# A DiT block with product-key experts on one core: gate steps dealt out one by one, eight one-hot row buffers, and U tiles fed in halves between the W steps

## The chip, the cores and the metric

The kernel runs on one core of a Trainium2 chip. The metric is the device time of one execution in microseconds (us), from the profiler's side of the chip; lower is better. The engines are PE (TensorE, matmul), DVE (VectorE), ACT (ScalarE), POOL (GpSimd) and SP (SyncE, which here only issues loads). Each works off its own queue strictly in order.

## What is computed

A block of a diffusion transformer for 256 tokens of width 2048: adaptive layer norm, a mixer of a gated MLP and a differential attention, and a feed-forward layer of 16384 experts, of which each token takes 16 for each of 8 heads. The change touches only the last. Cut to what matters, the reference is:

```python
def peer_ffn(h, wq, keys, u_tab, v_tab):            # blocks of 128 tokens, 8 heads
    q = (ht @ wq).reshape(128, 8, 2, 128)
    s = einsum('thcd,hcnd->thcn', q, keys)          # scores against 2 x 128 keys a head
    s_a, i_a = top_k(s[:, :, 0], 16); s_b, i_b = top_k(s[:, :, 1], 16)
    top_s, pos = top_k(all 16 x 16 sums of s_a and s_b, 16)
    idx = (i_a * 128 + i_b) at pos                  # expert a * 128 + b
    gate = softmax(top_s)
    act = gelu(einsum('thkd,td->thk', u_tab[idx], ht))
    return einsum('thk,thkd->td', gate * act, v_tab[idx])

x_new = x_new + g2 * peer_ffn(h2, ...)              # g2: sixth part of silu(c) @ w_ada + b_ada
```

## The kernel before

Ahead of the experts the kernel computes adaptive norms, mixer and output projection, some 630 us, which no part of the change touches. Then come three stages.

**Selection** (about 640 to 885 us). The loop over `j` in 0 to 15 makes one half head's query tile an iteration: `q_tile(j)` multiplies two 512 KB halves of `wq[j]` with h2 (48 matmuls, lines 130 to 132, tile z; the first two tiles are made ahead of the loop). `scores` (L812) multiplies the tile of the iteration before with the keys, and `topk` takes its 16 best on DVE (L790 to L798). At every fourth score tile `lookup` turns positions into experts: a chain that goes from DVE to POOL (L866, L870, L879) and back several times, with an exponential on ACT (L846). The iterations in the list `UJ` (0, 2, 4, 5, 7, 8, 9, 11 to 15) also make one U tile, `u_tile`: 128 experts' rows of u_tab times h2 for the first 192 tokens (TD), 16 pairs of matmuls (lines 135 and 136, tiles n and m). So iterations 1, 3, 6 and 10 have none. `xn_rows` writes rows of x back in the first eight iterations (transposes at L713).

In the same loop `adaln_g2` works out the gate vector g2. It has 32 steps of four traced matmuls (L265), one for each half megabyte of w_ada, and a piece is fetched through POOL's queue (L257) into one of two halves of a buffer. The fetch for step n+2 is issued when step n has read its half; a step that is asked for ends by issuing it. From iteration 2 on, two steps are taken in even iterations and three in odd ones, all ahead of `q_tile`.

All weights come through SP's queue into five raw buffers of 512 KB; `split` (L125, L126) makes a high part of each on ACT, a cast, and a low part on DVE, raw minus high. PE needs both. Three buffers of each exist.

**W stage** (about 885 to 1022). For each of the 192 tokens one matmul (L1016) makes a 128 x 128 table of gates, from a one-hot row block `ob` (four tokens at a time, by DVE at L1009 or by ACT at L1006 and L1007) and a one-hot row `pa` times the gate (L1014), which DVE and POOL make in turn. Six `pa` buffers go round. Four tokens fill a bank z, which ACT copies out (L1017); every 16 tokens a megabyte goes to DRAM. Between them U tiles 17 to 31 are made, a whole tile whenever enough tokens have passed, so that both run side by side.

**U and V** (from about 1022). The rest of the U tiles, the product of gates and activations, and the V tiles; the 64 rows of tokens not covered by TD are gathered and worked off on DVE. The output is written at the end.

The order on each engine isn't the order of the code: a list scheduler places instructions by the code's order as priority, by its own estimate of durations, and with splits raised by 400 places (HP). What it made of the code stands below as rows of the order.

Of the kernel before, what the change touches and what calls it, by code (L numbers as in the profile page):

```python
# [10 lines left out]
F32 = mybir.dt.float32  # L11
# [9 lines left out]
P = 128  # L21
# [8 lines left out]
NE = 128  # L30
# [3 lines left out]
LAG = 32  # L34
TB = 16
TD = 192
# [25 lines left out]
WP = 2  # L62
# [6 lines left out]
def dit_block(ctx: ExitStack, tc: tile.TileContext, xT, ctxT, cT, wad1, wada, bada, n1g, n2g,  # L69
# [15 lines left out]
    work = phase.enter_context(tc.tile_pool(name="work_a", bufs=1))  # L85

    def big(shape, dt=F32):
        return bigp.tile(shape, dt, tag="big", name="big")
# [4 lines left out]
    def w1(shape=(P, T), dt=F32):  # L93
        return work.tile(list(shape), dt, tag="w1", name="w1", bufs=4)
# [7 lines left out]
    def z512():  # L102
        return psz.tile([P, 512], F32, tag="z", name="z")
# [16 lines left out]
    def split(src, raw=None):  # L120
        raw = raw or load(src)
        hi = splp.tile([P, 1024], F32R, tag="hi", name="hi")
        lo = splp.tile([P, 1024], F32R, tag="lo", name="lo")
        with tc.high_priority(offset=HP):
            hi_at[0] = S.copy(hi, raw)  # L125
            anchor[0] = V.tensor_sub(lo, raw, hi)  # L126
        return hi, lo

    def mm3(ps, ah, al, bh, bl, first, last):
        mm(ps, ah, bh, start=first, stop=False)  # L130
        mm(ps, ah, bl, start=False, stop=False)  # L131
        mm(ps, al, bh, start=False, stop=last)  # L132

    def mm2(ps, wh, wl, act, first, last, n=T):
        mm(ps[:, :2 * n], wh, act[:, :, :n], start=first, stop=last)  # L135
        mm(ps[:, :n], wl, act[:, 0, :n], start=False, stop=last, skip_group_check=True)  # L136

    def fold(ps, dst, n=T):
        t = w1([P, n])
        S.copy(t, ps[:, n:2 * n])  # L140
        V.tensor_tensor(dst, ps[:, :n], t, op=ALU.add)
# [110 lines left out]
    def adaln_g2(buf):  # L252
        acc = z512()

        def fetch(n):
            if n < 2 * KT:
                G.dma_start(buf[:, n % 2], wada[3, n // 2, n % 2])  # L257

        for n in range(2):
            fetch(n)  # L260
        for n in range(2 * KT):
            k, i = n // 2, n % 2
            for jj in range(2):
                g = 32 * (2 * i + jj)
                mm(acc[g:g + 32, :], cs[:, k, :], buf[:, i, jj * 512:(jj + 1) * 512], start=(k == 0),  # L265
                   stop=(k == KT - 1))
            fetch(n + 2)
            yield
        S.copy(g2s, acc)
# [115 lines left out]
    def tok_chunk(c, tl, nfill):  # L385
        ps = {t: z512() for t in tl}
        for k2 in range(8):
            tok_part(c, k2, tl, ps)
            if k2 % 2:
                fill(3, nfill[k2 // 2])  # L390
        return ps
# [73 lines left out]
    for c in range(2):  # L465
        ps = tok_chunk(2 + c, (0, 1, 2, 3), FV)
# [58 lines left out]
    def feat_half(src, act8, ps, first, last, wide=True, n=T):  # L525
        hi, lo = split(src)
        for kk in range(8):
            wh, wl = hi[:, kk * P:(kk + 1) * P], lo[:, kk * P:(kk + 1) * P]
            f, l = first and kk == 0, last and kk == 7
            if wide:  # L530
                mm2(ps, wh, wl, act8[:, kk], f, l, n)
            else:
                mm3(ps[:, :n], wh, wl, act8[:, kk, 0, :n], act8[:, kk, 1, :n], f, l)

    def feat_chunk(src, act, ps, wide=True, n=T):
        for half in range(2):
            feat_half(src[half], act[half], ps, half == 0, half == 1, wide, n)
# [122 lines left out]
    for g in range(4):  # L660
        ps = {}
        for kh in range(2):
            for jp in (2 * g, 2 * g + 1):
                for i in range(2):
                    j = 2 * jp + i
# [42 lines left out]
    def xn_rows(b):  # L708
        tp = z512()
        for t in range(TT):  # L710
            for i in range(2):
                c = (2 * t + i) * P
                nc.tensor.transpose(tp[:, c:c + P], xn[:, 2 * b + i, t * P:(t + 1) * P], ident)  # L713
        xr = work.tile([P, TT, T], F32, tag="ob", name="xr", bufs=3)
        S.copy(xr, tp.rearrange("p (t d) -> p t d", t=TT))
        nc.scalar.dma_start(xd[:, :, b * T:(b + 1) * T], xr)

    h2 = [big([P, 8, 2, T], F32R) for _ in range(2)]
# [50 lines left out]
    work = phase.enter_context(tc.tile_pool(name="work_b", bufs=1))  # L769
# [30 lines left out]
    def q_tile(j):  # L800
        if j < WP:
            return wqp[j]
        ps = z512()
        feat_chunk(wq[j], h2, ps, False)
        qp = w1()
        S.copy(qp, ps[:, :T])
        return qp
# [77 lines left out]
    def gel_tile(a):  # L885
        if a % NG == 0:
            gel[a // NG] = gep.tile([P, NG, TD], F32, tag="ge", name="ge")
        return gel[a // NG][:, a % NG, :]

    def u_bank(a):  # L890
        return (m512 if a % 2 and a >= len(UJ) else n512)()

    def u_tile(a):
        if a >= NE:
            return
        ps = u_bank(a)
        feat_chunk(ut[a], h2, ps, True, TD)
        fold(ps, gel_tile(a), TD)

    u_next = 0  # L900


# [13 lines left out]
    def topk(j, qp):  # L916
        scores(j, qp)
        if j % 2:
            cands(j // 2)
        if j % 4 == 3:  # L920
            lookup(j // 2 - 1, 2)
            late_rows.append(j // 2 - 1)
        elif j % 4 == 1 and late_rows:
            rows_of(late_rows.pop(0))
# [28 lines left out]
    pend = []  # L953
    g2 = adaln_g2(gb0[:, 1].rearrange("p (i c) -> p i c", i=2))
    for j in range(16):
        if j >= WP:
            for _ in range(2 + j % 2):
                next(g2, None)
        pend.append((j, q_tile(j)))
        if len(pend) > DL:  # L960
            topk(*pend.pop(0))
        if j < 8:
            xn_rows(j)
        if j == 11:
            gb1 = big([P, 2, D])
            gbufs += [gb0[:, 1], gb1[:, 0], gb1[:, 1]]
        if j in UJ:
            u_tile(u_next)
            u_next += 1
# [18 lines left out]
    u_base = u_next  # L988
# [7 lines left out]
    wd = dram.tile([P, TD // TB, NE, TB], F32, tag="wd", name="wd", bufs=1)  # L996
    stg = big([P, 2, NE, TB])
    NTB = TD // TB
    for tb in range(NTB):
        st = stg[:, tb % 2]  # L1000
        for t4 in range(TB // 4):
            t0 = tb * TB + t4 * 4
            ob4 = work.tile([P, 4, P], F32, tag="ob", name="ob", bufs=3)
            if t4 % 2:
                for i in range(4):
                    S.activation(ob4[:, i, :], iota, AF.Abs, scale=-1.0, bias=eT[:, 1, t0 + i:t0 + i + 1])  # L1006
                S.activation(ob4, ob4, AF.Relu, scale=-1.0, bias=1.0)  # L1007
            else:
                V.tensor_tensor(ob4, iota[:, None, :].to_broadcast([P, 4, P]),  # L1009
                                eT[:, 1, t0:t0 + 4, None].to_broadcast([P, 4, P]), op=ALU.is_equal)  # L1010
            ps = z512()
            for i in range(4):
                pa = work.tile([P, P], F32, tag="pa", name="pa", bufs=6)
                (G if i % 2 else V).tensor_scalar(pa, iota, eT[:, 0, t0 + i:t0 + i + 1], eT[:, 2, t0 + i:t0 + i + 1],  # L1014
                                op0=ALU.is_equal, op1=ALU.mult)
                mm(ps[:, i * P:(i + 1) * P], ob4[:, i, :], pa, start=True, stop=True)  # L1016
            S.copy(st[:, :, t4 * 4:t4 * 4 + 4], ps.rearrange("p (t a) -> p a t", t=4))  # L1017
            while u_next < u_base + (t0 + 4) * (LAG - u_base) // TD:
                u_tile(u_next)
                u_next += 1  # L1020
        nc.scalar.dma_start(wd[:, tb], st)

    wts = {}
# [1 line left out]
    def w_load(gr):  # L1025
        if gr >= NE // NG:
            return
        wt = wtp.tile([P, NTB, NG, TB], F32, tag="wt", name="wt")
        nc.scalar.dma_start(wt, wd[:, :, gr * NG:(gr + 1) * NG, :])
        wts[gr] = wt  # L1030
# [27 lines left out]
        with tc.issue_after(hi_at[0].ins):  # L1058
            w_load(gr + 1)

    def u_steps():
        for a in range(u_next, NE):
            ps = u_bank(a)
            for half in range(2):
                feat_half(ut[a][half], h2[half], ps, half == 0, half == 1, True, TD)
                if half:
                    fold(ps, gel_tile(a), TD)
                yield a - 1 + half

    def v_unit(gr, dq, gt, between):  # L1070
        pa, pb = z512(), z512()
        for pr in range(4):
# [9 lines left out]
        return pa, pb  # L1082

    NGR = NE // NG
    w_load(0)
    ws = w_steps(0)
    for i in range(UX):
# [5 lines left out]
            next(ws, None)  # L1093
    phase.close()
    work = phase.enter_context(tc.tile_pool(name="work_c", bufs=1, reuse_waits="tile"))
    us = u_steps()
    done, wst = [0, 0, 0], [None]
    want = [2 * (NE - u_next), 2 * GT - rows_done[0]]

# [19 lines left out]

    for gr in range(NGR):  # L1120
        gt = gts.pop(gr)
        last = gr == NGR - 1
        if last:
# [3 lines left out]
        for dq in range(4):  # L1127
# [3 lines left out]
            ps = v_unit(gr, dq, gt, between)  # L1131
# [109 lines left out]
```

## Time and profile before

| | us |
|---|---|
| median of 3 runs (2083.24 to 2087.3) | 2086.74 |
| the profiled execution's own time | 2087.58 |
| its span, first to last instruction | 2085.7 |
| PE busy in the span | 1974.5 (95%) |
| DVE busy | 1638.9 (79%) |
| ACT busy | 1008.4 (48%) |
| POOL busy | 405.8 (19%) |
| mean granted clock of PE | 0.987 |

In a timeline row stand the start in us, the busy time of the group, the engine, the line, the operation, the tile written and those read, shapes, and the count; a number in square brackets is the time that the engine sat idle ahead of it, and behind the arrow what ended that. PE runs a float32 matmul of this kernel as two records where it isn't in the float32r format (L265, L713, L812, L1016). A granted clock of 1.00 is 2.4 GHz, 0.50 is 1.2 GHz.

### The profile page before, as it was taken

What the parts mean: (1) busy time and instruction counts of PE and PEld (TensorE: products, weight loads), DVE (VectorE), ACT (ScalarE), POOL (GpSimd) and SP (SyncE); (2) the same over time, 40 slices, a digit from 0 to 9 for tenths busy, and PEclk for the clock granted to TensorE, in tenths of its full rate; (3) what the DMA queues carried; (4) which work ended last, traced back from release to release, by engine and by line L of the source; (5) the groups of instructions that cost most, each with busy time, mean ns of one, the idle gap of its engine ahead of it and who ended that gap; (6) DMA issues with size and microseconds to landing.
All of it is one profiled execution on the core that took longest, in us unless ns stands there. A gap on an engine that the chain in (4) does not pass through costs nothing.

```text
span 2085.7 us, 29831 instructions
## 1 busy us (share of the span) xinstructions
PE 1974.5 (95%) x11182; PEld 1638.0 (79%) x11182; DVE 1638.9 (79%) x2344; ACT 1008.4 (48%) x1393; POOL 405.8 (19%) x315
## 2 busy tenths in 40 slices
PE   4999999999998888889999999999999999999998
PEld 1457775566997777888888898989898888888876
DVE  5338657677667677866698999999999899999997
ACT  3224314565556333377655555545554455445543
POOL 0001000000000232177412222222222223232200
PEclk9999999999999999899999999999999999999999
DMA  8787677776566676556799999999999999999984
GB/s 326 268 310 234 203 256 265 235 252 230 195 204 224 225 270 206 171 193 209 240 369 374 375 367 381 383 377 374 374 377 362 368 362 370 388 361 369 399 324 160
DMA packets 173744, 622.03 MB, mean 298 GB/s; under 512 B 17824, under 2 KB 44704, under 8 KB 154528
## 3 DMA queue, kind: packets, MB, share of 16 engines
q1 hardware_dynamic: 119232, 434.16, 58.7%
q0 software_dynamic: 23040, 151.01, 18.6%
q10 hardware_dynamic: 31328, 34.97, 4.9%
q8 instruction: 87, 1.43, 0.3%
q14 instruction: 57, 0.47, 0.1%
HBM read 603.30 MB, written 16.78 MB: 297 GB/s over the span
## 4 chain that ended last, share of the span: by engine, by line
PE 44%; DMA 3%; DVE 3%; issue 1%; ACT 0%; DVEq 0%; ACTq 0%
PE n L135 6%; PE m L135 6%; PE z L131 5%; PE z L130 5%; PE z L132 5%; PE z L1079 5%; PE z L1080 5%; PE n L136 3%; PE m L136 3%; DVE lo L126 2%; DMA raw<-in_vt 2%; DMA raw<-in_ut 1%; ACT hi L125 0%; DVE big L948 0%; DVE big L1155 0%
## 5 line engine op out<-in xcount | busy, mean ns | idle before, releaser
L125 ACT CAST hi<-raw 128x1024 fp32r<-128x1024 f32 x656 | 688.9, 1050 | 886.4 <-PE z L1079 166.1
L126 DVE TENSOR_TENSOR lo<-raw,hi 128x1024 fp32r<-128x1024 f32 x656 | 798.2, 1229 | 273.9 <-ACT hi L125 267.3
L135 PE MATMUL n<-big,hi 128*128 128x384 f32 x1120 | 334.4, 363 | 0.4 <-DVE big L733 0.2
L136 PE MATMUL n<-big,lo 128*128 128x192 f32 x1120 | 285.5, 255 | 6.4 <-DVE lo L126 6.2
L135 PE MATMUL m<-big,hi 128*128 128x384 f32 x928 | 275.5, 361 | 0.0
L130 PE MATMUL z<-hi,big 128*128 128x512 f32 x608 | 248.2, 409 | 4.5 <-DVE vtok L468 3.2
L131 PE MATMUL z<-lo,big 128*128 128x512 f32 x608 | 244.1, 402 | 4.0 <-DVE lo L126 3.8
L132 PE MATMUL z<-hi,big 128*128 128x512 f32 x608 | 240.1, 398 | 0.0
L136 PE MATMUL m<-big,lo 128*128 128x192 f32 x928 | 236.3, 255 | 0.7 <-DVE lo L126 0.7
L136 PEld LDWEIGHTS n<-big,lo 128*128 128x128 f32 x1120 | 216.5, 193 | 12.5 <-DVE lo L126 9.1
L135 PEld LDWEIGHTS n<-big,hi 128*128 128x128 f32 x1120 | 212.7, 190 | 5.4 <-DVE big L733 1.6
L932 POOL DMA_INDIRECT big<-in_vtab,iu x64 | 130.1, 2032 | 364.2 <-DVE big L948 336.7
L136 PEld LDWEIGHTS m<-big,lo 128*128 128x128 f32 x928 | 178.9, 193 | 6.1 <-DVE lo L126 2.9
L932 POOL DMA_INDIRECT big<-in_utab,iu x64 | 108.4, 1694 | 384.3 <-DVE big L940 375.1
L135 PEld LDWEIGHTS m<-big,hi 128*128 128x128 f32 x928 | 175.9, 190 | 3.5
L130 PEld LDWEIGHTS z<-hi,big 128*128 128x128 f32 x608 | 115.4, 190 | 50.8 <-issue 21.7
L130 PE MATMUL z<-big,hi 128*128 128x256 f32 (+1 forms) x512 | 147.9, 290 | 0.0
L948 DVE SCALAR_TENSOR_TENSOR big<-big,gate 128x2048 f32<-128x2048 f32 x63 | 147.7, 2345 | 0.0
L131 PE MATMUL z<-big,hi 128*128 128x256 f32 (+1 forms) x512 | 146.7, 287 | 0.1
L132 PE MATMUL z<-big,lo 128*128 128x256 f32 (+1 forms) x512 | 146.3, 286 | 0.0
L940 DVE SCALAR_TENSOR_TENSOR big<-big 128x2048 f32<-128x2048 f32 x64 | 146.2, 2284 | 0.0
L131 PEld LDWEIGHTS z<-lo,big 128*128 128x128 f32 x608 | 116.0, 191 | 36.3 <-DVE lo L126 9.1
(280 smaller groups left out, 3270.4 us busy)
## 6 DMA issues: line engine op xcount, KB each, us to landing
raw<-in_ut SPq DMA_DIRECT2D x256, 512.0 KB
raw<-in_vt SPq DMA_DIRECT2D x256, 512.0 KB
ra<-in_wada SPq DMA_DIRECT2D x96, 512.0 KB
raw<-in_wkvq SPq DMA_DIRECT2D x64, 512.0 KB
raw<-in_wad SPq DMA_DIRECT2D x42, 512.0 KB
raw<-in_wout SPq DMA_DIRECT2D x32, 512.0 KB
raw<-in_wq SPq DMA_DIRECT2D x32, 512.0 KB
big<-in_wada POOLq DMA_DIRECT2D x32, 512.0 KB, 7.4
```

The lines of the kernel that those rows point to most:

```text
L125: hi_at[0] = S.copy(hi, raw)
L126: anchor[0] = V.tensor_sub(lo, raw, hi)
L130: mm(ps, ah, bh, start=first, stop=False)
L131: mm(ps, ah, bl, start=False, stop=False)
L132: mm(ps, al, bh, start=False, stop=last)
L135: mm(ps[:, :2 * n], wh, act[:, :, :n], start=first, stop=last)
L136: mm(ps[:, :n], wl, act[:, 0, :n], start=False, stop=last, skip_group_check=True)
L932: G.indirect_dma_start(out=gbufs[n % 3], out_offset=None, in_=(utab if n < GT else vtab), in_offset=bass.IndirectOffsetOnAxis(ap=iu[:, s:s ...
L940: V.scalar_tensor_tensor(buf, buf, 1.0, hrow, op0=ALU.mult, op1=ALU.mult, accum_out=dots[:, s:s + 1])
L948: V.scalar_tensor_tensor(hrow, buf, gate[:, s:s + 1], hrow, op0=ALU.mult, op1=ALU.add)
L1079: mm(pb, g, hi[:, sl], start=(i == 0), stop=False)
L1080: mm(pb, g, lo[:, sl], start=False, stop=(i == NG - 1))
```

## The change

Three things. (1) The gate steps: instead of two or three ahead of `q_tile` from iteration 2 on, one stands ahead of it and one behind it in each of the 16 iterations; 32 in all, as before. (2) `pa` gets eight buffers. (3) The generator `u_steps`, which made U tiles in halves in the last stage, moves up and also serves the W stage: 30 halves instead of 15 whole tiles, each as soon as its share of tokens is done.

```diff
--- before.py
+++ after.py
@@ -897,6 +897,15 @@
         feat_chunk(ut[a], h2, ps, True, TD)
         fold(ps, gel_tile(a), TD)
 
+    def u_steps(a0, a1):
+        for a in range(a0, a1):
+            ps = u_bank(a)
+            for half in range(2):
+                feat_half(ut[a][half], h2[half], ps, half == 0, half == 1, True, TD)
+                if half:
+                    fold(ps, gel_tile(a), TD)
+                yield a - 1 + half
+
     u_next = 0
 
 
@@ -953,10 +962,9 @@
     pend = []
     g2 = adaln_g2(gb0[:, 1].rearrange("p (i c) -> p i c", i=2))
     for j in range(16):
-        if j >= WP:
-            for _ in range(2 + j % 2):
-                next(g2, None)
+        next(g2, None)
         pend.append((j, q_tile(j)))
+        next(g2, None)
         if len(pend) > DL:
             topk(*pend.pop(0))
         if j < 8:
@@ -996,6 +1004,7 @@
     wd = dram.tile([P, TD // TB, NE, TB], F32, tag="wd", name="wd", bufs=1)
     stg = big([P, 2, NE, TB])
     NTB = TD // TB
+    wu, w_done = u_steps(u_next, LAG), 0
     for tb in range(NTB):
         st = stg[:, tb % 2]
         for t4 in range(TB // 4):
@@ -1010,14 +1019,14 @@
                                 eT[:, 1, t0:t0 + 4, None].to_broadcast([P, 4, P]), op=ALU.is_equal)
             ps = z512()
             for i in range(4):
-                pa = work.tile([P, P], F32, tag="pa", name="pa", bufs=6)
+                pa = work.tile([P, P], F32, tag="pa", name="pa", bufs=8)
                 (G if i % 2 else V).tensor_scalar(pa, iota, eT[:, 0, t0 + i:t0 + i + 1], eT[:, 2, t0 + i:t0 + i + 1],
                                 op0=ALU.is_equal, op1=ALU.mult)
                 mm(ps[:, i * P:(i + 1) * P], ob4[:, i, :], pa, start=True, stop=True)
             S.copy(st[:, :, t4 * 4:t4 * 4 + 4], ps.rearrange("p (t a) -> p a t", t=4))
-            while u_next < u_base + (t0 + 4) * (LAG - u_base) // TD:
-                u_tile(u_next)
-                u_next += 1
+            while w_done < 2 * (LAG - u_base) * (t0 + 4) // TD:
+                next(wu)
+                w_done += 1
         nc.scalar.dma_start(wd[:, tb], st)
 
     wts = {}
@@ -1058,15 +1067,6 @@
         with tc.issue_after(hi_at[0].ins):
             w_load(gr + 1)
 
-    def u_steps():
-        for a in range(u_next, NE):
-            ps = u_bank(a)
-            for half in range(2):
-                feat_half(ut[a][half], h2[half], ps, half == 0, half == 1, True, TD)
-                if half:
-                    fold(ps, gel_tile(a), TD)
-                yield a - 1 + half
-
     def v_unit(gr, dq, gt, between):
         pa, pb = z512(), z512()
         for pr in range(4):
@@ -1082,6 +1082,7 @@
         return pa, pb
 
     NGR = NE // NG
+    u_next = LAG
     w_load(0)
     ws = w_steps(0)
     for i in range(UX):
@@ -1093,7 +1094,7 @@
             next(ws, None)
     phase.close()
     work = phase.enter_context(tc.tile_pool(name="work_c", bufs=1, reuse_waits="tile"))
-    us = u_steps()
+    us = u_steps(u_next, NE)
     done, wst = [0, 0, 0], [None]
     want = [2 * (NE - u_next), 2 * GT - rows_done[0]]
```

On POOL, around the first lookup (L257 fetches for gate steps, L866 to L879 are the lookup), before:

```order
L257 DMA big<-in_wada 128x1024 x9
L866 TENSOR_TENSOR oh<-oh,tabs 128x512
L870 TENSOR_TENSOR oh<-oh,s_5827 128x256 x2
L257 DMA big<-in_wada 128x1024 x2
L866 TENSOR_TENSOR oh<-oh,tabs 128x512
L870 TENSOR_TENSOR oh<-oh,s_5827 128x256
L879 TENSOR_TENSOR oh<-oh,big 128x256 x2
L870 TENSOR_TENSOR oh<-oh,s_5827 128x256
L257 DMA big<-in_wada 128x1024
L879 TENSOR_TENSOR oh<-oh,big 128x256 x2
```

and now:

```order
L257 DMA big<-in_wada 128x1024 x12
L866 TENSOR_TENSOR oh<-oh,tabs 128x512
L870 TENSOR_TENSOR oh<-oh,s_5836 128x256 x2
L257 DMA big<-in_wada 128x1024
L866 TENSOR_TENSOR oh<-oh,tabs 128x512
L870 TENSOR_TENSOR oh<-oh,s_5836 128x256 x2
L879 TENSOR_TENSOR oh<-oh,big 128x256 x2
L257 DMA big<-in_wada 128x1024
L879 TENSOR_TENSOR oh<-oh,big 128x256 x2
L257 DMA big<-in_wada 128x1024 x4
```

Twelve fetches instead of nine stand ahead of the lookup, and one instead of two behind its first part.

On PE, where one iteration ends and the next begins (L132 and L130 are the end and the start of a query tile, L812 scores, L265 a gate step), before:

```order
L132 MATMUL z<-big,lo 128x256
L812 MATMUL m<-big,w_5539 128x128 x2
L713 MATMUL z<-ident,big 128x128 x4
L265 MATMUL z<-big,cs 32x512 x2
L130 MATMUL z<-big,hi 128x256
L131 MATMUL z<-big,hi 128x256
L132 MATMUL z<-big,lo 128x256
L130 MATMUL z<-big,hi 128x256
L265 MATMUL z<-big,cs 32x512 x2
L131 MATMUL z<-big,hi 128x256
```

and now:

```order
L265 MATMUL z<-big,cs 32x512 x2
L812 MATMUL m<-big,w_5548 128x128 x2
L713 MATMUL z<-ident,big 128x128 x4
L265 MATMUL z<-big,cs 32x512 x2
L130 MATMUL z<-big,hi 128x256
L131 MATMUL z<-big,hi 128x256
```

One step stands behind the old tile and one ahead of the next; none is left inside a tile. The first four steps now stand at the front, among the transposes of h2 (L740).

On ACT, in the middle of the W stage (L125 the high part, L1017 and L1026 the copy of a bank, L1006 and L1007, now L1015 and L1016, the row blocks), before:

```order
L125 CAST hi<-raw 128x1024
L1007 ACTIVATE ob<-ob 128x512
L125 CAST hi<-raw 128x1024
L140 COPY w_8405<-m 128x192
L1017 COPY big<-z 128x128x4
L1006 ACTIVATE ob<-iota,big 128x128 x2
L1017 COPY big<-z 128x128x4
L1006 ACTIVATE ob<-iota,big 128x128 x2
L1007 ACTIVATE ob<-ob 128x512
L1017 COPY big<-z 128x128x4
```

and now:

```order
L125 CAST hi<-raw 128x1024
L1026 COPY big<-z 128x128x4
L1015 ACTIVATE ob<-iota,big 128x128 x2
L1016 ACTIVATE ob<-ob 128x512
L1015 ACTIVATE ob<-iota,big 128x128 x3
L1016 ACTIVATE ob<-ob 128x512
L125 CAST hi<-raw 128x1024
L140 COPY w_8301<-n 128x192
L1026 COPY big<-z 128x128x4 x2
L1015 ACTIVATE ob<-iota,big 128x128 x4
```

The two casts of a tile, which stood almost side by side, now stand one by one between copies. On PE the W matmuls stood in runs of ten and two or twelve, with a U tile of 32 matmuls behind them; now they stand in runs of eight and four with 16 between. SP's loads keep their order throughout, and behind the last W matmul the order is as before on every engine but for one place on ACT and DVE right behind it.

## Rows read from the trace of the kernel before

**Rows 1.** Stretches: length, busy PE, PEld, DVE, ACT, POOL, granted clock, DMA share, GB/s.
```profile
640.00:885.00 245.00, 212.40 (x1451) 183.51 (x1451) 179.12 (x618) 92.06 (x148) 55.68 (x73) 0.93 0.65 222
885.00:1022.00 137.00, 121.24 (x850) 113.14 (x851) 83.92 (x168) 100.79 (x214) 98.30 (x96) 1.00 0.60 201
1022.00:2085.70 1063.70, 1046.32 (x5672) 922.17 (x5670) 970.64 (x932) 538.14 (x589) 233.48 (x125) 1.00 0.95 360
```

**Rows 2.** Waits of PE, 640 to 885, then 885 to 1022; total, times, longest.
```profile
PE z L265 <- DMA big<-in_wada: 24.3, 9, 6.6
PE n L136 <- DVE lo L126: 4.4, 2, 3.1
...
PE z L1016 <- POOL pa L1014: 10.2, 17, 0.8
PE z L1016 <- DVE pa L1014: 3.2, 5, 0.7
```

**Rows 3.** Timeline of PE, 660 to 830: start, us, engine, line, operation, tiles, count.
```profile
668.54 1.05 PE L265 MATMUL z<-big,cs 128*32 128x512 f32 x4 [0.43 <-DMA big<-in_wada]
...
676.51 1.05 PE L265 MATMUL z<-big,cs 128*32 128x512 f32 x4 [2.06 <-DMA big<-in_wada]
...
682.84 0.60 PE L812 MATMUL m<-big,w 128*128 128x128 f32 x4
...
688.37 1.07 PE L265 MATMUL z<-big,cs 128*32 128x512 f32 x8
...
698.93 1.92 PE L265 MATMUL z<-big,cs 128*32 128x512 f32 x4 [6.55 <-DMA big<-in_wada]
...
710.30 1.06 PE L265 MATMUL z<-big,cs 128*32 128x512 f32 x8
...
734.77 1.07 PE L265 MATMUL z<-big,cs 128*32 128x512 f32 x8
...
741.60 0.60 PE L812 MATMUL m<-big,w 128*128 128x128 f32 x4
...
767.99 1.07 PE L265 MATMUL z<-big,cs 128*32 128x512 f32 x8
...
797.43 0.61 PE L812 MATMUL m<-big,w 128*128 128x128 f32 x4
...
824.70 1.07 PE L265 MATMUL z<-big,cs 128*32 128x512 f32 x8
```

**Rows 4.** Timeline of POOL, 660 to 700; then what line 257's transfers took.
```profile
669.91 0.53 POOL L257 DMA_DIRECT2D big<-in_wada  x1 [4.22 <-PE z L265]
...
692.32 1.39 POOL L866 TENSOR_TENSOR oh<-oh,tabs 128x512 bf16<-128x512 bf16 x1 [13.92 <-DVE oh L856]
...
694.92 1.11 POOL L257 DMA_DIRECT2D big<-in_wada  x2
...
DMA to landing us min/median/max: 3.9/7.4/10.0
```

**Rows 5.** Timeline of DVE behind the first and the second lookup's scores.
```profile
696.26 2.67 DVE L126 TENSOR_TENSOR lo<-raw,hi 128x1024 fp32r<-128x1024 f32 x1
...
764.11 1.23 DVE L126 TENSOR_TENSOR lo<-raw,hi 128x1024 fp32r<-128x1024 f32 x1 [1.55 <-ACT hi L125]
```

**Rows 6.** Busy time of each engine behind the fourth lookup, columns as in Rows 1.
```profile
860.00:877.00 17.00, 14.30 (x51) 13.51 (x52) 12.62 (x19) 3.20 (x4) 6.34 (x7) 0.50 0.41 130
```

**Rows 7.** Timelines of PE, POOL, DVE and ACT in one round of the W stage.
```profile
942.51 2.29 PE L1016 MATMUL z<-pa,ob 128*128 128x128 f32 x18
945.64 0.49 PE L1016 MATMUL z<-pa,ob 128*128 128x128 f32 x2 [0.84 <-POOL pa L1014]
...
943.24 6.17 POOL L1014 TENSOR_SCALAR pa<-iota,big 128x128 f32<-128x128 f32 x6 [2.17 <-PE z L1016]
...
943.70 1.23 DVE L126 TENSOR_TENSOR lo<-raw,hi 128x1024 fp32r<-128x1024 f32 x1
...
942.62 1.04 ACT L125 CAST hi<-raw 128x1024 fp32r<-128x1024 f32 x1 [0.71 <-PE n L135]
```

## The prediction

> **What bounds the kernel now.** I read the busy time by stretch first, then the waits of PE in the two stretches that the change touches, then the timelines around those waits. In [rows 1] PE is busy 1046.32 of the last 1063.70 us, in which its order stays as it was: there is nothing to win there, and whatever is won ahead of 1022 us should reach the end. The expert selection (640 to 885) leaves PE 32.6 of 245 us idle, at a mean granted clock of 0.93; the W stage (885 to 1022) leaves 15.8 of 137. [rows 2] names the causes. In the selection 24.3 us, in 9 waits, are gate steps (L265) that wait for their half megabyte of w_ada; only 4.4 us are waits for a low part. In the W stage 10.2 us are waits for a one-hot row from POOL, 3.2 for one from DVE.
>
> **Why a gate step waits.** The gate matrix streams through two half buffers, so the fetch for step n+2 is issued when step n has left its half. In [rows 3] the step at 668.54 frees a half, POOL issues at 669.91 [rows 4], and the step at 676.51 uses it after 2.06 us of idling: 8.0 us from step to step, 6.6 of them from issue to landing. The median landing is 7.4 us [rows 4], which makes 8.8. The old code puts two steps side by side, then has nothing to do with them for a tile, then wants a third. It is worse at a lookup: POOL works off its queue in order, and at 692.32 it has sat 13.92 us before L866, waiting for DVE; the fetch behind it leaves at 694.92, and PE idles 6.55 us before the step at 698.93 [rows 3, 4]. Two more lookups meet gate steps in the same way.
>
> The Trainium skill gives a price for such a fetch ("DMA: Bandwidth & Descriptors", section "Anatomy of one DMA"): some 2 us plus the bytes at 436 GB/s, an estimate of 3.2 us for 512 KB. By that price every wait of singly dealt steps would vanish, and the time would be some 5 us lower, about 2063 and inside the forecast below; the trace's 6.6 and 7.4 us decide against it, and the sum below goes by them.
>
> **The change, gate steps.** Prices from [rows 3]: two steps take 1.07 us, so one 0.5; from 734.77 to 741.60 stand two steps and a query tile, so the tile is 5.8; from 682.84 to 688.37 stand scores, transposes and a U tile, 5.5, of which I put 0.9 on the eight small matmuls ahead of it (0.60 busy for the four of the scores) and 4.6 on the U tile. With one step on each side of the query tile an iteration takes 12.3 us with a U tile and 7.7 without. Step n+2 stands one iteration behind step n. Against 8.0 to 8.8, iterations with a U tile never wait; the three without one that lie in the middle (3, 6, 10) wait 0.3 to 1.1. I walk the new order through, as time from one mark to the next:
>
> Front, up to the scores at 682.84. Four steps now stand in iterations 0 and 1, among the h2 transposes, with some 4 to 5 us of PE work between step 0 and step 2, and as much between 2 and 4; at 8 us that is two waits, about 2.5 and 2.3, then 0.8 and 0.3 at iterations 3 and 4. Gone are 0.43 and 2.06. Three more steps have been done by then (1.5 us). Together +4.9; but PE has waits of its own in the h2 stretch (32.6 us of idling less the 24.3 and 4.4 of [rows 2] leaves 3.9, nearly all there), which the front waits swallow: I take 0, with +5 kept for the range.
>
> Lookups. What decides after the change is no longer the fetch: it leaves POOL about 12 us behind the scores and is wanted some 24 us behind them. It is DVE's chain, which the change doesn't shorten. From the second lookup's scores (741.60) it is free for the last low part of the U tile behind the next query tile at 762.56 (764.11 less the 1.55 it waited for ACT), so +22.2 with its 1.23 [rows 5]. Half a U tile (2.3) later PE is at the next step: +24.5. Now that mark is reached at 767.99, +26.4. For the first and third lookups it is 710.30 and 824.70, +27.5 and +27.3 [rows 3]. At the first, the low part of the query tile's second half comes at 698.93, +16.1 [rows 5], which still leaves room. Gains 3.0, 1.9 and 2.8: 7.7 in all; the rest of the waits for w_ada there turns into waits for low parts.
>
> Between lookups. 710.30 to 741.60 is 31.3 us; iterations 6, 7 and the first half of 8 are 7.7 + 12.3 + 6.8, with 1 us of waits 27.8: 3.5 less. 767.99 to 797.43 is 29.4; by the same walk 27.3: 2.1 less. Behind the last mark two more steps stand than before: +1.
>
> Sum of the gate part: 0 - 7.7 - 3.5 - 2.1 + 1 = -12.3. The clock takes part back: PE still idles 2 to 5 us inside each lookup, and behind the fourth lookup such idling went with a granted clock of 0.50, the level of 1.2 GHz [rows 6]. My marks have PE at full clock; some of the loss hides under DVE's waits, so I charge 0.9 per lookup: **-9.6**. Bounds: -14 without a drop and with the h2 stretch covering all; +8 if each lookup loses 6 us more (the first rival).
>
> **The change, W stage.** Now PE runs ten or twelve W matmuls and then the rest of a U tile. Nine matmuls (two records each) take 2.29 us [rows 7], 0.254 each; POOL makes six rows in 6.17, 1.03 each, and supplies every second matmul, so a run eats a POOL row per 0.51 us. Six buffers hold three of POOL's rows: the run outlives them, PE waits 0.84 at its tenth matmul, and POOL, with its buffers full, had just waited 2.17 for PE [rows 7]. Afterwards the order has runs of eight and four with half a U tile (2.3 us) between them, and eight buffers hold the whole of the longest run. Per 20 matmuls PE needs 20 x 0.254 + 3 x 2.32 = 12.0 us and POOL 10 x 1.03 = 10.3: POOL keeps up by 1.7 us per round. Left is the first filling of the ring, some 3.4 us by the same walk. The two extra buffers add no instruction. The next tightest is ACT, 100.79 us busy in [rows 1], 79% of a stage of about 128: its cast of a half now stands between copies that wait for PE, but two halves ahead of its use, so I charge 1.0 us for it. Of the 13.4 us of [rows 2] (10.2 and 3.2) remain 4.4: **-9.0**; bounds -13 and 0.
>
> SP's order of loads is unchanged instruction for instruction. Behind the W stage everything stands as before, so I count no loss there; DMA is 0.95 busy in that stretch, and no more data is moved.
>
> **Sum.** 2087.58 (the profiled run) - 9.6 - 9.0 = 2069.0. That run was 0.84 above the median of the three, so the forecast against the median is 2068.
>
> **The rivals.**
> Lookups take it back: PE idles in each lookup, falls to 0.50 and stays there as it does behind the fourth lookup, which has no gate step in it: 17 us at 0.50 [rows 6], with 4.4 us of waits for low parts [rows 2]. Half of 17 is 8.5 us, 6 more than the 2.5 that each of the three loses now. The gate part becomes -9.6 + 18 = +8, the time 2087 with the W stage's gain. For it: the chain is the same. Against it: behind the fourth the U tiles come without a query tile between them, so they ask for a half every 2.3 us. Chance 0.06.
>
> The fetches come late all the same: if each landed at the 10.0 us of [rows 4] (11.4 from step to step), iterations with a U tile still hold, the three others wait 3 us more each and the front's two 3.4: gate part +6, time 2085. Chance 0.05.
>
> POOL and DVE exclude each other in the W stage: if each low part (1.23 us, three per 20 matmuls) stopped POOL for its length, a round would be 10.3 + 3.7 = 14.0 us, and 192 matmuls 9.6 x 14.0 = 134, where PE's work of 118.4 and the 13.4 make 132 now; time 2080. Against it: POOL's six rows in [rows 7] keep 1.03 each although the low part at 943.70 falls among them. The Trainium skill has this as a rule ("SBUF — State Buffer", section "Two separate sides"): a GpSimd operation and a DVE operation with two SBUF inputs lock each other out. This trace does not bear it out for these two operations, though at the first lookup a low part beside POOL's work took 2.67 [rows 5]. Chance 0.07.
>
> Slower than before: ACT sets the W stage. If the copies that wait for PE hold up the cast, each of the 30 halves of the stage's 15 U tiles waits for cast and low part, up to 1.04 + 1.23 = 2.3 us [rows 7]. PE's own work there is 192 x 0.254 + 15 x 4.64 = 118.4 us, so the stage would take 118.4 + 30 x 2.3 = 187 instead of 132, and the kernel 2133. It is slower than before from 0.8 us per half on. Against it: the cast's place two halves ahead. Chance 0.05.
>
> It doesn't do what it says: the scheduler could have moved the steps back together. The order rows show them apart; chance nil.
>
> **Chances.** Forecast (2057 to 2078) 0.74, with a further 0.03 below it; POOL 0.07, lookups 0.06, fetches 0.05, ACT 0.05. The range 2057 to 2081 takes in the forecast and POOL, 0.81. A measurement of this kernel can tell about 0.2% (4 us) from no change. Faster by more than that: the forecast and what is below it, POOL, and half of the fetches: 0.86. Within: the lookups and the other half, 0.08. Slower: 0.06, ACT and a rest.
>
> **What would show it.** Right: waits of L265 for w_ada under 10 us, none over 3; waits for low parts in 640 to 885 risen from 4.4 to 10 us or more; POOL waits in the W stage under 4 us; the last W matmul some 20 us earlier, and the stretch behind it as long as before. Wrong: waits for w_ada still over 15 us (landing, not placing, was the limit); ACT named before PE in the W stage; or a stretch behind 1022 that grew by what was won.

## The result, and the profile of the changed kernel

| | before | changed |
|---|---|---|
| median of four runs, us | 2084.99 | 2054.26 |
| lowest to highest, us | 2082.96 to 2087.3 | 2050.24 to 2058.74 |
| the profiled execution, us | 2087.58 | 2050.24 |
| its span, us | 2085.7 | 2048.3 |
| mean granted clock of PE | 0.987 | 0.994 |

The ratio is 0.9842 (the medians alone give 0.9853), with a 95% interval of 0.9817 to 0.9866: 28 to 38 us faster. The two profiled executions lie 37.3 us apart, more than the medians' 30.7, and sums taken from the two traces below belong to the 37. The forecast was 2068 with a range of 2057 to 2081, a gain of 18.6. The direction was right, the gain nearly twice as large, and the time fell 3 us below the range. A second set of runs, on another occasion beside the kernel before, gave 0.9836.

The stretches of the changed kernel that answer to [rows 1] (selection, W stage, all behind it), in the same columns:

```profile
640.00:871.00 231.00, 215.38 (x1458) 180.53 (x1456) 179.44 (x617) 95.65 (x150) 56.48 (x72) 0.98 0.70 235
871.00:986.00 115.00, 112.39 (x860) 110.89 (x859) 84.64 (x169) 99.72 (x213) 104.92 (x96) 1.00 0.70 238
986.00:2048.30 1062.30, 1044.84 (x5661) 919.96 (x5659) 969.42 (x931) 537.22 (x588) 234.23 (x125) 1.00 0.95 360
```

The selection is 14 us shorter, with a granted clock of 0.98 in place of 0.93; the W stage is 22 us shorter, and PE idles 2.6 us of its 115; the rest is as long as before. POOL is now busy 104.92 of 115 us in the W stage, the fullest engine next to PE.

The waits of PE in 640 to 871 of the changed kernel, to be held against [rows 2]: gate steps no longer appear, and waits for low parts have grown from 4.6 (4.4 and a further 0.2 on tile m) to 13.8 us.

```profile
PE n L136 <- DVE lo L126: 10.5, 5, 3.1
PE z L132 <- DVE lo L126: 2.4, 2, 1.2
...
PE m L136 <- DVE lo L126: 0.9, 1, 0.9
```

The W stage is better read in PE's weight loads (PEld), which run ahead of the matmuls. First the kernel before, 885 to 1022, then the changed one, 871 to 986 (its line 1025 is line 1016 of before, 1023 is 1014):

```profile
PEld z L1016 <- POOL pa L1014: 17.1, 31, 1.0
PEld z L1016 <- DVE pa L1014: 4.4, 5, 0.9
PEld z L1016 <- ACT ob L1007: 1.3, 1, 1.3
```

```profile
PEld z L1025 <- POOL pa L1023: 1.8, 4, 0.8
PEld z L1025 <- DVE pa L1023: 0.9, 1, 0.9
PEld z L1025 <- ACT ob L1016: 0.9, 1, 0.9
```

By these rows PE stood 22.8 us in the W stage before, not the 14 that its matmul rows show, and stands 3.6 now.

### The profile page after: what moved, and what is told of

Same layout as the page of the kernel before. It is cut to its first block, busy times and chain, and to the rows that moved or that the text cites. A ratio compares the mean times of both kernels' runs of the same rounds, so it can differ in the third digit from the quotient of the medians.

```text
span 2048.3 us, 29826 instructions
## 1 busy us (share of the span) xinstructions
PE 1965.5 (96%) x11182; PEld 1626.8 (79%) x11182; DVE 1638.8 (80%) x2344; ACT 1009.4 (49%) x1393; POOL 414.9 (20%) x315
## 4 chain that ended last, share of the span: by engine, by line
PE 75%; DVE 11%; DMA 9%; issue 2%; ACT 2%; POOL 1%; ACTq 0%; DVEq 0%; POOLq 0%
PE z L131 10%; PE z L130 10%; PE z L132 10%; PE n L135 9%; PE m L135 7%; PE z L1079 5%; PE z L1080 5%; DVE lo L126 4%; DMA ra<-in_wada 4%; PE n L136 4%; PE m L136 3%; PE z L1025 2%; DMA raw<-in_vt 2%; DMA raw<-in_ut 2%; PE n L237 2%
## 5 line engine op out<-in xcount | busy, mean ns | idle before, releaser
L125 ACT CAST hi<-raw 128x1024 fp32r<-128x1024 f32 x656 | 688.6, 1050 | 859.7 <-PE z L1079 163.3
L130 PE MATMUL z<-hi,big 128*128 128x512 f32 x608 | 246.6, 406 | 2.7 <-DVE vtok L468 1.7
L132 PE MATMUL z<-hi,big 128*128 128x512 f32 x608 | 238.5, 395 | 0.0
L130 PEld LDWEIGHTS z<-hi,big 128*128 128x128 f32 x608 | 114.2, 188 | 48.6 <-issue 21.0
L132 PE MATMUL z<-big,lo 128*128 128x256 f32 (+1 forms) x512 | 144.5, 283 | 2.4 <-DVE lo L126 2.4
L130 PE MATMUL z<-big,hi 128*128 128x256 f32 (+1 forms) x512 | 145.7, 286 | 0.0
L131 PE MATMUL z<-big,hi 128*128 128x256 f32 (+1 forms) x512 | 144.3, 282 | 0.1
L132 PEld LDWEIGHTS z<-hi,big 128*128 128x128 f32 x608 | 114.1, 188 | 33.9 <-issue 8.7
```

## Experiments: the two parts apart

The kernel before with the new gate loop alone:

```diff
-        if j >= WP:
-            for _ in range(2 + j % 2):
-                next(g2, None)
+        next(g2, None)
         pend.append((j, q_tile(j)))
+        next(g2, None)
```

> The kernel before with the gate steps alone dealt out singly (W stage as before: six row buffers, whole U tiles). Theory: the gate part is worth what stands ahead of the first W matmul in the changed kernel, 888.13 to 873.74, 14.4 us, whatever the W stage does: about 2071 against 2085; no wait of a gate step for w_ada over 1 us, each fetch landing in 3.7 to 4.1 us (before: 3.9/7.4/10.0), PE busy with L265 some 8 us more than before (35 against 27.5), since a step alone takes 0.98 us and two side by side 0.99. Rival, the sizes of the forecast: 9.6 us, 2075, the rest of the 30.7 coming from the two parts together.

Measured: 0.993 of the time before (0.9906 to 0.9955), 14.6 us with an interval of 9.4 to 19.7. Busy time in L265 rose to 35.4 us, waits for w_ada fell to 1.7. The interval holds both the theory's 14.4 and the forecast's 9.6, so time alone doesn't choose between them. Two of the theory's smaller claims were missed: the longer of the two waits left was 1.03 us, and the fetches, singly as they were, landed in 3.7/4.9/9.7 us (least, median, most) instead of 3.7 to 4.1.

The other half, the changed kernel with the old gate loop (the diff above the other way round, in the changed kernel):

> The changed kernel with the old gate loop (two or three steps ahead of the query tile from iteration 2 on), so the W stage's part alone: eight row buffers and U halves. Theory: PE's real waits in the W stage of before were the 22.8 us of the weight loads, not the 13.4 us of the matmul rows, and nearly all go: 21 to 23 us, about 2062 to 2064; from the first to the last W matmul 110 to 112 us instead of 131.9. Rival, the forecast's size: 9.0 us, 2076, stage about 122.

Measured: 0.9883 (0.9857 to 0.9909), 24.5 us, interval 19.0 to 29.9. The forecast's 9.0 is excluded. From the first to the last W matmul it took 110.3 us, against 131.6 before. The two halves make 39.1 us, the whole 33 to 34 (0.9842 and 0.9836): within their intervals they add up, and no interaction between them is needed.

Then the two edits of the W stage one by one. The kernel before with eight row buffers only:

```diff
-                pa = work.tile([P, P], F32, tag="pa", name="pa", bufs=6)
+                pa = work.tile([P, P], F32, tag="pa", name="pa", bufs=8)
```

> The kernel before with eight one-hot row buffers in place of six, and nothing else: U tiles still whole, gate steps as before. The W stage's part of the change is worth about 23 us. Theory: POOL's rows run dry in runs of ten or twelve W matmuls; two more buffers are one more of POOL's rows in stock, some 1.03 us of its work per run, so about 60% of the waits for pa go (POOL waits of the weight loads 17.1 to about 7): 11 to 15 us, 2071 to 2075 against 2085 to 2090 for the kernel before in this batch. Rival: the ring is refilled only while a whole U tile runs, and the long runs set it: under 5 us.

And U halves only: the changed kernel with that line the other way round and the old gate loop.

> The changed kernel with the old gate loop and six row buffers: U tiles in halves between the W steps alone. Theory: with runs of eight and four, six buffers hold three of POOL's rows for the four that a run of eight eats, so a wait of about 0.5 us is left in the long runs only: the halves alone bring 14 to 19 us of the W stage's 23, about 2068 to 2073, POOL waits of the weight loads 17.1 to about 5. Rival: the two edits bring half each, 11 us.

Measured: 0.9918 (0.9891 to 0.9945), 17 us, and 0.99 (0.9865 to 0.9935), 21 us. The weight loads of the one-hot matmuls show what each edit leaves. Buffers alone, the row of the group and what ended its idle time:

```profile
L1016 PEld LDWEIGHTS z<-pa,ob x384: 186/192/192, 884.8 to 1002.8; 128*128 128x128 f32 x192
  POOL pa L1014: 8.9, 14
  ACT ob L1007: 3.0, 3
```

Halves alone:

```profile
L1026 PEld LDWEIGHTS z<-pa,ob x384: 186/192/192, 889.5 to 1004.4; 128*128 128x128 f32 x192
  POOL pa L1024: 4.5, 6
```

| | waits for POOL's rows, us | first to last W matmul, us |
|---|---|---|
| before | 17.1 | 131.6 |
| gate steps alone | 17.2 | 131.7 |
| eight buffers alone | 8.9 | 118.2 |
| halves alone | 4.5 | 115.0 |
| both (W part, and the changed kernel) | 1.9 and 1.8 | 110.3 |

Both edits came out near their expectation (7 us and 5 us of waits for POOL were expected, 8.9 and 4.5 came; the gains of 17 and 21 us lie above the 11 to 15 and 14 to 19 expected, with these inside or at the edge of the intervals). They cure the same waits, so they don't add up: 13.4 and 16.6 us of the stage apart, 21.3 together.

## Experiments: what a gate step costs, and what a fetch costs

The changed kernel, but both steps of an iteration side by side:

```diff
         next(g2, None)
+        next(g2, None)
         pend.append((j, q_tile(j)))
-        next(g2, None)
```

> The changed kernel, but both gate steps of an iteration stand side by side ahead of the query tile, in all 16 iterations: an even deal in pairs. Theory A (two steps side by side use different column groups of PE and cost what one costs; fetches go one after another at 4.0 us): PE's time in L265 falls from 35.5 to about 17 to 20; the second fetch of each pair lands at about 8 us, the first at 4; 8 us are less than an iteration with a U tile, so only the iterations without one wait, 1 to 3 us each: 4 to 8 us of waits for w_ada, time about 2043 to 2048. Theory B (a step costs PE the same alone or in a pair, and spreading the steps is the whole gain): no gain in L265, waits for w_ada of 8 us or more, time 2058 to 2065, slower than the changed kernel.

Measured: 0.9776 (0.9738 to 0.9813), median 2043.24. Because this beat the changed kernel, the two ran again beside each other:

> The changed kernel again, beside the next one on the same chip: 0.984 of the time before, 2050 to 2058.

> The changed kernel with both gate steps of an iteration side by side ahead of the query tile, again, on the same chip as the changed kernel. Theory (two steps side by side cost PE what one costs): 8 to 14 us under the changed kernel, 0.977 to 0.980 of the time before. Rival (the 11 us of the first run were chance): within 4 us of the changed kernel.

Measured: the changed kernel 0.9836 (0.9811 to 0.986), the pairs 0.9803 (0.9778 to 0.9828), 7 us less; the theory's 8 is just missed, and these two intervals overlap. The traces carry it: from a matmul of line 130 ahead of the selection (at 526.89 us in the changed kernel) to the first W matmul the pairs took 343.1 and 341.6 us, the changed kernel 346.8 and 348.4, so some 5 us are real. What theory A said of PE is shown by steps that nothing holds up. The changed kernel's timeline of PE, start, us, engine, line (a step, then scores right behind it):

```profile
694.68 1.05 PE L265 MATMUL z<-big,cs 128*32 128x512 f32 x4
695.66 0.71 PE L812 MATMUL m<-big,w 128*128 128x128 f32 x4
```

One step has PE for 0.98 us, from its start to that of the scores. In the kernel before two steps together had 1.07 [rows 3]: they use different column groups of PE. Dealt out singly, the 32 steps make PE's busy time in L265 35.5 us instead of 27.5. In pairs it is 23.5, more than the 17 to 20 expected, since in the early iterations pairs still come apart. The waits for w_ada, put at 4 to 8 us by theory A, were 1.8 and 1.5 us in the two executions. The Trainium skill has the mechanism ("TensorE: Matmul & The Clock Gate", section "Part 3: Packing small matmuls — row/col tiling"): matmuls on distinct column groups run at the same time. The rows here agree.

The same experiment shows what a fetch costs, and that theory A priced it wrongly. Its POOL issues two fetches at 664.81, and the second is what the second step waits for:

```profile
664.81 1.05 POOL L257 DMA_DIRECT2D big<-in_wada  x2 [11.60 <-PE z L265]
```

```profile
671.24 1.05 PE L265 MATMUL z<-big,cs 128*32 128x512 f32 x4
672.53 1.05 PE L265 MATMUL z<-big,cs 128*32 128x512 f32 x4 [0.23 <-DMA big<-in_wada]
```

This pair was complete 7.7 us behind its first issue, which looks like one fetch standing behind the other at 3.9 us each. Other pairs of the same run don't bear that out (DMA share: busy share of the DMA engines from the first issue to the second landing):

| first issue | landing of the first, of the second, us from its own issue | pair complete, us | DMA share |
|---|---|---|---|
| 691.45 | 4.1, 4.8 | 5.3 | 0.76 |
| 664.81 | 4.0, 7.2 | 7.7 | 0.85 |
| 725.81 | 10.8, 12.7 | 13.3 | 0.95 |

Nor does a fetch alone always take 4.0 us. The summary of [rows 4] (3.9/7.4/10.0) rests on four of the 32 fetches, for which the trace of the kernel before has a landing: 8.8 us from 647.38, 3.9 from 702.06, 10.0 from 736.14 and 6.0 from 777.56, with DMA shares of 0.93, 0.66, 1.01 and 0.79. The longest was the first of its pair. The trace of the changed kernel also has four (3.7 to 4.1); its second execution has all 32, dealt singly:

```profile
DMA to landing us min/median/max: 3.7/5.0/10.4
```

The 10.4 is the fetch issued at 729.40, at a DMA share of 1.01. The fetch before it had landed (728.00), but two row gathers that POOL had issued were still on their way (until 737.37), and two loads through SP's queue beside it took 8.9 and 9.2 us. The fetch at 746.96 landed in 4.0, at 0.67. So long landings go with busy DMA engines; how much of one is the order of POOL's queue and how much the load beside it isn't shown. Long or short, the gate steps of that execution waited only 0.3 us.

Last, a step on all four column groups, so that it is short without a partner:

```diff
-            for jj in range(2):
-                g = 32 * (2 * i + jj)
-                mm(acc[g:g + 32, :], cs[:, k, :], buf[:, i, jj * 512:(jj + 1) * 512], start=(k == 0),
-                   stop=(k == KT - 1))
+            for jj in range(4):
+                g = 32 * jj
+                mm(acc[g:g + 32, i * 256:(i + 1) * 256], cs[:, k, :], buf[:, i, jj * 256:(jj + 1) * 256],
+                   start=(n == 0), stop=(n == 2 * KT - 1))
```

> The changed kernel with every gate step as four matmuls of 256 columns, one for each of the four column groups, in place of two of 512 on two groups (the gate row is then read back from the bank in that order; same sums, same fetches, steps dealt singly as in the changed kernel). Theory: the groups work side by side, so a single step takes about 0.5 us instead of 0.98, 32 x 0.48 = 15 us less of PE in L265 (35.5 to about 20), and the time falls by 8 to 15 us to 2039 to 2046, less where a lookup's chain of DVE and POOL ends last anyway. Rival: what counts is the number of matmuls or the weight loads (four in place of two), and a step still takes about 1 us: 2054, the same as the changed kernel.

Measured: 0.9826 (0.98 to 0.9852), not distinguishable from the changed kernel's 0.9842 and 0.9836. The mechanism holds, the gain doesn't. A step has PE for 0.57 us (its own timeline):

```profile
690.75 0.64 PE L265 MATMUL z<-big,cs 128*32 128x256 f32 x8
691.32 0.71 PE L812 MATMUL m<-big,w 128*128 128x128 f32 x4
```

and L265's busy time is 22.5 instead of 35.5 us, 13 less. Where these went is seen when the selection is cut at the scores that begin a lookup and at the prediction's mark, the gate step that follows the U tile behind the next query tile, in us:

| stretch | before | changed | gate alone | four groups | pairs |
|---|---|---|---|---|---|
| first lookup: scores to mark | 27.5 | 22.0 | 21.0 | 23.9 | 23.8 |
| to the second lookup's scores | 31.3 | 31.4 | 32.6 | 28.1 | 28.2 |
| second lookup | 26.4 | 20.5 | 21.0 | 24.2 | 20.8 |
| to the third lookup's scores | 29.4 | 31.2 | 30.7 | 28.1 | 28.4 |
| third lookup | 27.3 | 20.5 | 21.5 | 22.3 | 20.8 |
| to the first W matmul | 63.4 | 66.1 | 67.4 | 65.7 | 65.9 |
| sum | 205.3 | 191.6 | 194.2 | 192.2 | 187.7 |

Between lookups the short steps win 3 us each time. Within the lookups they lose 1.9, 3.7 and 1.8, because PE gets sooner to a low part that DVE delivers no sooner: in the second lookup it is ready 19.9 us behind the scores, in the changed kernel 18.2. The second lookup of this kernel, against that of the changed kernel (the row ahead of the mark, and the mark):

```profile
750.54 0.53 PE L136 MATMUL n<-big,lo 128*128 128x192 f32 x1 [2.96 <-DVE lo L126]
754.74 1.08 PE L265 MATMUL z<-big,cs 128*32 128x256 f32 x8
```

```profile
753.64 0.36 PE L136 MATMUL n<-big,lo 128*128 128x192 f32 x1 [1.97 <-DVE lo L126]
755.94 1.05 PE L265 MATMUL z<-big,cs 128*32 128x512 f32 x4
```

The wait is 1.0 longer, and behind it the half tile takes 4.2 us instead of 2.3, which with the 1.8 us of DVE makes the 3.7: the same matmul shows 0.53 instead of 0.36 us. The granted clock from 752.00 to 754.70 was 0.50, the level of 1.2 GHz, where the changed kernel had 1.00 (753.00 to 756.00); from 745.00 to 750.00, ahead of the fall, PE had been busy 2.54 of 5 us, at 0.99. That is the first rival of the prediction in small. That the lookups' chain is what took the gain back is read from one trace of this kernel; it was not tested by a run of its own.

## Why the prediction was right and wrong, step by step

**W stage, forecast 9.0, measured 21.3 in the trace and 24.5 (19.0 to 29.9) in the run of this part alone.** This term makes up nearly the whole miss. The mechanism was right: POOL's rows run dry in the long runs, two buffers and shorter runs cure it, and 3.6 us are left where 4.4 were forecast. The size was wrong at two places. The waits of [rows 2] were taken as PE's idle time: 13.4 us. A matmul row's end is modelled, and a W matmul's tail covers part of the next one's wait; the weight loads, which have no such tail, waited 22.8 us. The Trainium skill warns of the matmuls' busy share ("Perfetto Trace Analysis", section "Identifying the Most-Contended Engine"): pipelined matmuls make it a bad measure of how full TensorE is, and it names the weight loads' busy share among the better ones. Here the same holds for waits: 13.4 us by the matmuls, 22.8 by the weight loads, 21.3 won. What hid the error is that the sum closed by chance: PE's work was put at 192 x 0.254 plus 15 U tiles, 118.4, and 13.4 of waits made the 132 of the stage. But 0.254, from a run of W matmuls that itself waited for rows [rows 7], is too dear, and by the order of instructions only 219 of the 240 pairs of U matmuls of these tiles (16 a tile) stand between the first and the last W matmul. In the changed kernel, where a run of eight and half a U tile follow one another without a wait, and then a run of four and half a tile, the timeline has

```profile
904.92 1.97 PE L1025 MATMUL z<-pa,ob 128*128 128x128 f32 x16
...
908.98 1.08 PE L1025 MATMUL z<-pa,ob 128*128 128x128 f32 x8
```

and the next run starts at 912.17. Eight and a half tile take 4.06 us, four and a half tile 3.19, so four W matmuls take 0.87, or 0.22 each, and half a tile 2.32. PE's work in the stage of before is then 192 x 0.22 + 219/8 x 2.32 = 106 us, and some 26 of its 131.6 were idle. In the changed kernel, where 225 pairs stand there, the same prices make 107 of its 110.3.

**Gate part, forecast 9.6, measured 13.7 in the trace (14.4 with the front) and 14.6 (9.4 to 19.7) in the run of this part alone.** The sum was 4 to 5 us short, about at its bound of 14, but its terms were further off and partly cancelled:

- Front: forecast 0; the scores of the first lookup start at 682.10 instead of 682.84, 0.7 us earlier.
- Lookups: forecast +24.5 us from scores to mark in all three, a gain of 7.7; measured +22.0, +20.5 and +20.5 by the table, a gain of 18.2. That DVE's chain decides after the change, and that the change doesn't shorten it, was right. The failed step is the row that was taken for its end, "free for the last low part of the U tile" at 762.56. The low part at 764.11 [rows 5] isn't the U tile's. A query tile and a U tile take four low parts, and PE takes them in the order in which DVE makes them. Behind the scores at 741.60 DVE starts them at 742.75, 747.83, 753.12 and 758.24; the fifth, at 764.11, is for the query tile after that. In the changed kernel it is the fourth behind the scores that ends PE's wait in each of the three lookups (at 700.95, 753.64 and 805.31). The fourth of the second lookup, in the kernel before and in the changed one:

```profile
758.24 1.21 DVE L126 TENSOR_TENSOR lo<-raw,hi 128x1024 fp32r<-128x1024 f32 x1
```

```profile
751.88 1.70 DVE L126 TENSOR_TENSOR lo<-raw,hi 128x1024 fp32r<-128x1024 f32 x1
```

It ends 17.9 us behind the scores in the one and 18.2 in the other: the chain is as long as it was, and before the change PE came to it only at 765.6, long after its end. With half a U tile (2.3) behind it the right row gives +20.2 for the second lookup and for the third (its fourth low part runs from 814.06), as measured within 0.4, and +22.8 for the first (from 702.12), where 22.0 was measured. In the same way the low part at 696.26 [rows 5] is the U tile's first, not the query tile's second.
- Between lookups: forecast 3.5 and 2.1 less; measured 0.1 and 1.8 more. The failed step is "two steps take 1.07 us, so one 0.5": one takes 0.98, and an iteration with a U tile takes 13.1 us (scores at 774.01 to scores at 787.09) where 12.3 was priced. The second stretch also holds a wait of 1.2 for a low part of a query tile.
- Behind the last mark: forecast 1 more, measured 2.7 more, for the same reason.
- The clock: forecast a loss of 2.7. The granted clock of the selection rose instead, from 0.93 to 0.98; PE idles 15.6 us there instead of 32.6.
- The fetch: the 7.4 us behind "8.8 from step to step" were the middle of four known landings. Dealt singly, all 32 have a median of 5.0 in the second execution of the changed kernel, and hardly a step waits. The price of the Trainium skill that I set aside ("DMA: Bandwidth & Descriptors", section "Anatomy of one DMA"), an estimate of 3.2, was too low for every landing measured here (3.7 at least), but nearer to that median than 7.4.

**No loss behind the W stage:** right. From the last W matmul to the end 1065.9 us before, 1064.3 now; over all ten traces this stretch takes 1060 to 1074, so 1.6 says nothing.

**The rivals.** Lookups take it back: no, the three are shorter, though the kernel with steps on four groups shows the mechanism at work. Fetches land at 10 us: one did, with a median of 5.0. ACT sets the W stage: no, 0.9 us of waits. Each sign named beforehand came: no wait for w_ada ahead of L265's matmuls, low-part waits above 10 us, POOL waits under 4, and the last W matmul earlier, by 36 us instead of some 20.

POOL and DVE exclude each other in the W stage: they do, and I misread [rows 7]. Its six rows in 6.17 us are not six of 1.03. One by one they take 0.79, 1.57, 1.48, 0.82, 0.79 and 0.79 us, and the two long ones are those beside which DVE works on two tensors: the last 0.9 us of the low part from 943.70 in the one, a row block of 0.68 us in the other. In the changed kernel, two rows of POOL that follow one another, and DVE's low part within the first:

```profile
902.88 1.87 POOL L1023 TENSOR_SCALAR pa<-iota,big 128x128 f32<-128x128 f32 x1
904.74 0.79 POOL L1023 TENSOR_SCALAR pa<-iota,big 128x128 f32<-128x128 f32 x1
```

```profile
902.93 1.24 DVE L126 TENSOR_TENSOR lo<-raw,hi 128x1024 fp32r<-128x1024 f32 x1
```

Rows of POOL beside which DVE has no operation on two tensors have a median of 0.79 us (38 rows before, 30 in the changed kernel); those with 0.9 us or more of a low part beside them have 1.57 before (10 rows) and 1.80 now (17). The low parts keep their 1.23 (median 1.225 before, 1.226 now), so it is POOL that waits. The rival's price, 3.7 us a round on top of ten rows of 1.03, counted this twice, for the 1.03 has it in already. POOL's rows now take 1.10 on average, since more low parts fall among them.

## What to carry to other kernels

Judge a wait of PE by its weight loads as well as by its matmuls, and hold the sum against a count of the work between the same two instructions; a sum that closes can close by two errors. Before a row is taken as the one that PE will wait for, count which matmul reads it: here the fifth low part was taken for the fourth, which put the chain's end at 22.2 us instead of 17.9. Before a mean is taken as an operation's price, look at the operations one by one: 1.03 us was 0.79 and a wait. Before neighbours are dealt out singly, see whether they ran side by side: the pairs keep the even deal and PE's column groups, and came out ahead of the changed kernel, at 0.9776 and 0.9803 of the time before.

## What was not expected of the hardware

Half a megabyte fetched through POOL has no one price: it lands in 3.7 to 12.7 us. Two such fetches, issued 0.6 us apart, were complete in 5.3 us at a DMA share of 0.76 and in 13.3 at 0.95, so neither one figure nor a figure times the place in the queue foretells it.

DVE and POOL exclude each other, in the lookups as in the W stage, and either can be the one that waits. In the W stage it is POOL, by the rows above. In the lookups it can be DVE. In the kernel with steps on four groups a DVE operation on 128 x 32 elements, which elsewhere takes 0.18 us, took 1.73 and ended when POOL's operation did (at 743.8; the same in its first and third lookup, at 691.7 and 796.1):

```profile
742.13 1.73 DVE L872 TENSOR_TENSOR s<-s,s 128x32 f32<-128x32 f32 x1
```

```profile
742.61 1.18 POOL L866 TENSOR_TENSOR oh<-oh,tabs 128x512 bf16<-128x512 bf16 x1
```

The first 0.48 us of it, in which POOL issues a fetch, aren't explained by POOL's row. That the two exclude each other is the rule of the Trainium skill ("SBUF — State Buffer", section "Two separate sides"), and the rows of both stages agree. Why it is POOL in the one and DVE in the other wasn't tried.
